# RWKV stage of a hybrid decoder layer: PSUM banks dealt out anew, and norms, joins, inversion and gate jobs placed elsewhere in the order

## The chip, the cores and the metric

One core of a Trainium2 chip runs the kernel. The metric is device time in microseconds, the median of several runs; before the change it is 2560.88 us (2558.31 to 2565.73 over 3 runs). Beside these runs there is one profiled execution, from which every row below is read.

## What is computed

One layer of a decoder over a prompt of 1040 rows and 64 sample rows: an input projection, an mLSTM mixer, an RWKV-7 mixer, a merge of the two behind gates, an output projection and a conv FFN. The change touches the RWKV mixer:

```
S = S * w + sa (kk * a) + v k        (per head, state 64 x 64; sa = S . -kk)
y = S r
y = headnorm(y) * lnx_g + lnx_b + (sum r k r_k) v      (the "bonus")
hB = y * g                                             (gate from a LoRA)
merged = sigmoid(gA) hA + sigmoid(gB) hB
```

The reference steps through time one row after another; the kernel works in chunks of 64 rows, where the delta rule becomes a triangular system per head and chunk whose inverse is computed on VectorE.

## The kernel before

Phase 1 does norms, mLSTM and its projections, phase 2 the output projection and the FFN. Between them lies the recurrent stage, the method `rwkv`, some 1250 us long. Its rows come in three passes of 384 columns, its 16 heads in four groups of 4 (two head pairs, 128 partitions each): 12 steps `(pas, u)`. A loop n runs over the steps, from -2 to 12. In one turn of it, four things are laid side by side in 18 rounds:

- the chain (`rwkv_chain`) of step n: for each of 6 chunks three parts, one a round. Part one multiplies the state with the chunk's rows (`y<-S,RA`, `y<-VU,Gk`), part two solves with the inverse (`u<-Rs,TT`), and lets the next chunk's rows be transposed (`t<-cst,v`, `t<-cst,KB`), part three makes the state update (`u<-VU,KBT`) and the outputs (`y<-VU,Gr`), which DVE (L1044) adds into the state and ACT (L1046) copies into Yt.
- the preparation of step n+2 (`rwkv_g`, `rwkv_t`, `rwkv_mid`): chunk products G (`gg<-RA,KB`), read off by DVE into Gd, Gr and Gk (L809 to L818); the inversion on DVE, a chain of 30 pairs of products in LX (L842, L844) between a transpose of Gd (L835) and two of LX (T, L887 and L889); then two products with the inverse on PE (`gg<-T,A`), each in two halves, P1 with P2 and P3 with P4 here. Each generator yields the time, in turns, at which it wants to go on; those numbers (`t0` for the inversion, `m0` for the products) set where the work stands. Steps that open a pass are n = 0, 4 and 8 of the 12.
- the rear of step n-1 (`rwkv_back`): head norm, transposes (`t<-cst,Yt`), merge.
- dense projections, in units of three matmuls (hi x hi, lo x hi, hi x lo, `d<-X..`), 8 units to a job: k and r of step n+2 (`rwkv_k`, `rwkv_r`), v of step n+1, and gate jobs from one queue (`gates_b`, `gate_o`, `gate_a`). The list `ga` says how many gate jobs each turn takes, from n = -2 on. Small pieces (the gate's LoRA product, the bonus products) wait in the list `small` and are let in some units later.

PE's order is as the code is written (a manual schedule); a scheduler orders the other engines by priority. `rwkv_r` also makes the norm of kk on PE (`y<-cst,sq`) and the decay products on DVE.

PSUM has 8 banks: two `d` for dense work, one `t` for transposes, two `y` and one `u` for the chain, the norm, bonus and gate pieces, and one double bank `gg` for chunk products. The method `gbank` hands out `gg`; a new tile waits until the readers of the last one are done.

Of the kernel before, what the change touches and what calls it, by code (L numbers as in the profile page):

```python
# [14 lines left out]
P = 128  # L15
# [28 lines left out]
class Trunk:  # L44
# [89 lines left out]
    def setup(self):  # L134
        nc, tc, ctx, i = self.nc, self.tc, self.ctx, self.i
        self.cpool = ctx.enter_context(tc.tile_pool(name="cpool", bufs=1))
        self.dram = ctx.enter_context(tc.tile_pool(name="dram", bufs=1, space=bass.MemoryType.DRAM))
        self.wpool = ctx.enter_context(tc.tile_pool(name="wpool", bufs=1))
        self.psd = ctx.enter_context(tc.tile_pool(name="psd", bufs=2, space=bass.MemoryType.PSUM))
        self.pst = ctx.enter_context(tc.tile_pool(name="pst", bufs=1, space=bass.MemoryType.PSUM))  # L140
        self.psc = ctx.enter_context(tc.tile_pool(name="psc", bufs=1, space=bass.MemoryType.PSUM))
        c = self.cpool
        self.cst = c.tile([P, NCONST], F32, name="cst")
        self.xs_d = self.dram.tile([9, P, D], F32, name="xs_d")
        self.mA_d = self.dram.tile([8, P, 1152], F32, name="mA_d")
        self.gA_d = self.dram.tile([8, P, 1152], F32, name="gA_d")
        self.gB_d = self.dram.tile([8, P, 1152], F32, name="gB_d")
        self.o_d = self.dram.tile([8, P, 706], F32, name="o_d")
        self.x_d = [self.dram.tile([P, KT, 1114], F32, name=n) for n in ("xh_d", "xl_d")]
        self.mg_d = self.dram.tile([8, P, 1152], F32, name="mg_d")  # L150
# [80 lines left out]
    def gbank(self):  # L231

        self.complete()
        return self.psg.tile([P, 2, 512], F32, name="gg")

# [397 lines left out]
    def gates_b(self, pas, j, w, pool):  # L633

        nc, i = self.nc, self.i
        off = W * pas
        lw = self.wpool.tile([P, 512], F32, name="raw", bufs=3)[:, 0:128]
        nc.sync.dma_start(out=lw, in_=i["lora2"][j, :, 256:384])
        lh = pool.tile([P, 128], F32R, name="lwgh")
        ll = pool.tile([P, 128], F32R, name="lwgl")  # L640
        self.parts(lw, lh, ll, nc.gpsimd)
        th = pool.tile([P, W], F32, name="tho", bufs=3)
        yield from self.tanh_gate(pas, w, th)
        xg = self.xg

        def piece():
            ps = self.psc.tile([P, 512], F32, name="y", bufs=2)
            self.mm3(ps[:, :W], (lh, ll), xg, True, True)
            nc.vector.scalar_tensor_tensor(th, th, 1.0, ps[:, :W], op0=ALU.add, op1=ALU.mult)
            nc.sync.dma_start(out=self.gB_d[j, :, off:off + W], in_=th)  # L650

        self.small += [(self.cfg.get("b1", 4), piece)]
# [45 lines left out]
    def rwkv_r(self, pas, j, w, pool):  # L698
# [7 lines left out]
        act = nc.scalar.activation  # L706
        st = self.st[pas, j]
        r, k, a, b, lw = (st[n] for n in ("r", "k", "a", "b", "lw"))
        cw, Dt, ta = (pool.tile([P, W], F32, name=n) for n in ("cw", "Dt", "ta"))
# [33 lines left out]
        yield from units  # L743

        n2 = r_["n2"]
        ps = self.psc.tile([P, 512], F32, name="y", bufs=2)
        for p in range(NP):
            self.mm(ps[:, 2 * p:2 * p + 2], sq[:, p * 128:(p + 1) * 128], self.const("bones2"))
        c = slice(6 * m, 6 * m + 6)
        ts(n2[:, c].rearrange("p (h n) -> p n h", h=2), ps[:, 0:6].rearrange("p (n h) -> p n h", h=2), 1e-24, None, op0=ALU.max)  # L750
        nc.vector.reciprocal(n2[:, c], n2[:, c])
        if m:
            n2L = pool.tile([P, 32], F32, name="n2L", bufs=2)
            nc.vector.transpose(n2L, n2)
        yield
        DL = pool.tile([P, 16], F32, name="DL", bufs=6)
# [9 lines left out]
        tt(r, r, Dv, op=ALU.mult)  # L766
        st["DL"] = DL
        if m:
            self.un[pas, j // 2] = dict(n2L=n2L)
# [58 lines left out]
    def rwkv_t(self, pas, u, pool):  # L828
# [4 lines left out]
        g = self.r["Gd"][:, 0:384]  # L833
        yield self.cfg.get("t0", 0.87)
        nc.vector.transpose(LX, bass.AP(g.tensor, g.offset, [list(g.ap[0]), [12, 32], [1, 32]]))  # L835
        tt(LX, LX, n2L.unsqueeze(2).broadcast_to([P, 32, 32]), op=ALU.mult)
        nc.gpsimd.memset(LX.rearrange("p t s -> p (t s)")[:, 0:1024:33], 1.0)
        for s in range(1, 31):
            m = 31 - s
            tm = pool.tile([P, 240], F32, name="tm")  # L840
            tv_ = tm[:, 0:m * s].rearrange("p (t s) -> p t s", s=s)
            tt(tv_, LX[:, s + 1:, s:s + 1].broadcast_to([P, m, s]),  # L842
               LX[:, s:s + 1, 0:s].broadcast_to([P, m, s]), op=ALU.mult)
            tt(LX[:, s + 1:, 0:s], LX[:, s + 1:, 0:s], tv_, op=ALU.add)  # L844
            if s % 2 == 0:
                yield self.cfg.get("t0", 0.87) + self.cfg.get("tw", 0.75) * s / 30
        tt(LX, LX, n2L.unsqueeze(1).broadcast_to([P, 32, 32]), op=ALU.mult)
        yield self.cfg.get("t0", 0.87) + self.cfg.get("tw", 0.75)

    def rwkv_bonus(self, pas, j, pool):  # L850
# [13 lines left out]
        def piece():  # L864
            ps = self.psc.tile([P, 512], F32, name="y", bufs=2)
            for x in (hi, lo):
# [10 lines left out]
    def rwkv_mid(self, pas, u, pool):  # L877
# [5 lines left out]
        cs = slice(0, 12)  # L883
        m0 = self.cfg.get("m0", 1.78) if (pas, u) != (0, 0) else self.cfg.get("m00", 1.78)
        yield m0
# [3 lines left out]
        nc.vector.transpose(Tn, LX.rearrange("p t s -> p s t"))  # L889
        yield m0 + 0.1  # L890
        P1 = A21
# [20 lines left out]

        yield from (m0 + 0.12 for _ in product(A21, Tn, 0, 32, lambda w, h1: nc.scalar.copy(P1[h1], w[h1])))
        for q in (0, 64):
            nc.scalar.copy(TT[q:q + 32, 0, :, cs], Tx[q:q + 32, :, cs])
        nc.scalar.copy(TT[:, 1, :, cs], Tx[:, :, cs])
        yield m0 + 0.15
        yield from (m0 + 0.17 for _ in product(P1, Tx, 32, 0, lambda w, h0: nc.scalar.copy(
            TT[h0, 1, :, cs].rearrange("p t c -> p c t"), w[h0])))
        if pas == 0:  # L920

            yield m0 + 0.2
            for m, st in self.pairs(pas, u):
# [16 lines left out]
    def rwkv_chain(self, pas, u, pool):  # L940
# [30 lines left out]
        for p in range(NP):  # L971
            nxt = []
            for e in range(2):
# [5 lines left out]
                if not (smp or meta):  # L979
                    for m, st in prs:  # L980
                        sd = pool.tile([P, 128], F32, name="SD", bufs=4)
                        nc.scalar.activation(sd, S2[m], AF.Copy, scale=st["DL"][:, ch:ch + 1])
                        SD.append(sd)
                yr = self.psc.tile([P, 512], F32, name="y", bufs=2)
                yy, rr = yr[:, 0:128], yr[:, 128:256]
# [17 lines left out]
                yield  # L1003
                up = self.psc.tile([P, 512], F32, name="u")
                for h in range(2):
                    for m in range(2):
                        self.mm(up[brs[m], hh[h]], TT[brs[m], :, :, 6 * m + h * NP + p], Rs[brs[m], hh[h]])
                for m in range(2):
                    nc.scalar.copy(now[m][0][brs[m], e, :], up[brs[m], 0:128])
                if p + 1 < NP:  # L1010
# [12 lines left out]
                else:  # L1023
                    sp = self.psc.tile([P, 512], F32, name="u")
                    for m in range(2):
                        for h in range(2):
                            self.mm(sp[hh[h], 64 * m:64 * m + 64], now[m][1][:, e, hh[h]], now[m][0][:, e, hh[h]], skip=True)
                for h in range(2):
# [117 lines left out]
    def rwkv(self, steps):  # L1146

        self.st, self.un, self.tho, self.mt, self.rest = {}, {}, {}, {}, None
        i, N = self.i, len(steps)
# [21 lines left out]
        queue = [x for n in range(N) for x in gates(n)]  # L1171
        share = self.cfg.get("ga", [0] + [6] * 8 + [5, 5, 5, 9, 0, 0])

# [72 lines left out]
        for n in range(-2, N + 1):  # L1246
# [13 lines left out]
            for r in range(rounds):  # L1260
                if r == 12 and 0 <= n + 1 < N:
                    self.rwkv_bonus(steps[n + 1][0], 2 * steps[n + 1][1], pool)
# [4 lines left out]
                for m, x in inside.items():  # L1267
                    now = n + r / rounds - (m - 2)
                    while x[0] <= now and "n2L" in self.un.get(steps[m], ()):
                        x[0] = next(x[1], 9)  # L1270
                        if m in starts and x[0] < self.cfg.get("t0", 0.87):
                            x[0] = max(x[0], now + self.cfg.get("id", 0.05))
# [19 lines left out]
    def phase1(self, early, p1, rs):  # L1292
        tc, nc = self.tc, self.nc
        self.rs = rs
        self.normed = {}
        with tc.tile_pool(name="psg1", bufs=2, space=bass.MemoryType.PSUM) as self.psg, tc.tile_pool(name="m", bufs=1) as mp:
            self.mp = mp
# [32 lines left out]
        self.lo_eng = nc.gpsimd  # L1330
        with tc.tile_pool(name="psg2", bufs=1, space=bass.MemoryType.PSUM) as self.psg:
            with tc.manual_schedule(engines={mybir.EngineType.PE}):
# [3 lines left out]
    def phase2(self, early):  # L1336
# [3 lines left out]
        NX = 1090  # L1340
        with tc.tile_pool(name="psg3", bufs=2, space=bass.MemoryType.PSUM) as self.psg, tc.tile_pool(name="p2", bufs=1) as pp:
            X1h = pp.tile([P, KT, NX], F32R, name="X1h")
# [384 lines left out]
```

## Time and profile before

| What | Value |
|---|---|
| Median of 3 runs | 2560.88 us |
| The profiled execution | 2566.45 us, span 2564.7 us |
| PE busy, share of the span | 2385.6 us, 93% |
| DVE, ACT, POOL busy | 1549.9, 1085.7, 476.1 us |
| Mean granted clock of TensorE | 0.96 of full speed |

Busy times add up an engine's instructions; matmuls overlap, so PE's busy share says where it stood still rather than how full it was. The granted clock is a share of 2.4 GHz; it has two levels, 1.2 and 2.4 GHz, and a mean between them says how long each held.

### The profile page before, as it was taken

The page shows a single profiled execution, that of the slowest core. Times are in us where ns is not written, and L with a number is a line of the kernel's source. Part 1 is how long each engine was busy: PE and PEld are TensorE (multiplying, and loading weights), DVE is VectorE, ACT ScalarE, POOL GpSimd, SP SyncE. Part 2 cuts the span into 40 slices and gives each one's busy share as a digit, 9 for nine tenths or more (in the row PEclk, how much of TensorE's full clock was granted, in tenths as well). Part 3 has the DMA queues.
Part 4 walks back from the last instruction along what each step waited for, and adds up shares of the span by engine and source line. Part 5 has one row for each costly group of instructions (what it writes and reads, how often), then busy time and mean ns, then how long its engine had stood idle before and what let it go on. Part 6 is the DMA issues. An engine that isn't in the chain of part 4 may idle for free. (4 is left out here: it accounts for less than half of the span.)

```text
span 2564.7 us, 43729 instructions
## 1 busy us (share of the span) xinstructions
PE 2385.6 (93%) x16303; PEld 2148.3 (84%) x16303; DVE 1549.9 (60%) x3367; ACT 1085.7 (42%) x2454; POOL 476.1 (19%) x669
## 2 busy tenths in 40 slices
PE   6999998879899899999989999989999999999997
PEld 5888897768787788888878888888999999999996
DVE  7654545888885588765688874356434333343437
ACT  4443444435444456545646655445313222132222
POOL 5100014444553211101111212221000000000003
PEclk9998998889999899999999999989999999999999
DMA  8562534435448354557445566895211111021112
GB/s 277 174 174 82 181 122 127 161 122 174 132 155 262 110 167 158 175 176 247 143 159 163 165 205 212 267 318 181 62 29 62 36 47 47 32 63 33 50 38 81
DMA packets 212508, 356.97 MB, mean 139 GB/s; under 512 B 24626, under 2 KB 83890, under 8 KB 212295
## 3 DMA queue, kind: packets, MB, share of 16 engines
q1 hardware_dynamic: 212295, 354.17, 43.0%
q8 instruction: 129, 2.11, 0.3%
q14 instruction: 84, 0.69, 0.1%
HBM read 272.00 MB, written 82.08 MB: 138 GB/s over the span
## 5 line engine op out<-in xcount | busy, mean ns | idle before, releaser
L57 PE MATMUL d<-Xh,whi 128*128 128x384 f32 (+3 forms) x1544 | 557.8, 361 | 12.4 <-ACT sm L1142 3.7
L57 PE MATMUL d<-Xl,whi 128*128 128x384 f32 (+3 forms) x1544 | 531.0, 344 | 1.4 <-DMA Xl<-xl_d 0.9
L57 PE MATMUL d<-Xh,wlo 128*128 128x384 f32 (+3 forms) x1544 | 529.1, 343 | 2.4 <-DMA wlo<-lo_w_out_b 1.4
L57 PE MATMUL d<-X1h,whi 128*128 128x364 f32 (+2 forms) x1120 | 371.1, 332 | 3.5 <-ACT whi L90 3.4
L57 PE MATMUL d<-X1h,wlo 128*128 128x364 f32 (+2 forms) x1120 | 370.7, 331 | 0.0
L57 PE MATMUL d<-X1l,whi 128*128 128x364 f32 (+2 forms) x1120 | 370.2, 331 | 0.0
L57 PEld LDWEIGHTS d<-Xh,whi 128*128 128x128 f32 (+1 forms) x1544 | 302.3, 196 | 37.6 <-issue 8.8
L57 PEld LDWEIGHTS d<-Xl,whi 128*128 128x128 f32 (+1 forms) x1544 | 303.0, 196 | 6.1 <-DMA Xl<-xl_d 4.1
L57 PEld LDWEIGHTS d<-Xh,wlo 128*128 128x128 f32 (+1 forms) x1544 | 301.9, 196 | 5.5 <-DMA wlo<-lo_w_out_b 2.3
L73 ACT CAST whi<-raw 128x512 fp32r<-128x512 f32 (+1 forms) x255 | 157.0, 617 | 336.7 <-PE d L57 273.3
L57 PEld LDWEIGHTS d<-X1h,whi 128*128 128x128 f32 x1120 | 212.1, 189 | 8.0 <-ACT whi L90 3.9
L57 PEld LDWEIGHTS d<-X1l,whi 128*128 128x128 f32 x1120 | 212.0, 189 | 4.9
L57 PEld LDWEIGHTS d<-X1h,wlo 128*128 128x128 f32 x1120 | 212.2, 189 | 3.3
L90 ACT CAST whi<-raw 128x512 fp32r<-128x512 f32 x232 | 142.9, 618 | 137.5 <-PE d L57 75.7
L1550 DVE TENSOR_TENSOR acc<-y,acc 128x512 f32<-128x512 f32 (+1 forms) x144 | 97.6, 687 | 169.9 <-PE y L57 169.9
L74 POOL TENSOR_TENSOR wlo<-raw,whi 128x512 fp32r<-128x512 f32 x120 | 163.3, 1362 | 186.0 <-ACT whi L73 167.7
L74 DVE TENSOR_TENSOR wlo<-raw,whi 128x512 fp32r<-128x512 f32 (+1 forms) x135 | 97.0, 722 | 153.4 <-ACT whi L73 152.1
L844 DVE TENSOR_TENSOR LX<-LX,tm 128x30 f32<-128x30 f32 (+4 forms) x360 | 148.4, 412 | 9.8 <-DVE tm L842 0.5
L57 PE MATMUL y<-wdh,hh 128*128 128x512 f32 x352 | 138.9, 395 | 4.8 <-DVE acc L1550 4.8
L842 DVE TENSOR_TENSOR tm<-LX 128x30 f32<-128x30 f32 (+4 forms) x360 | 137.9, 383 | 8.8
L57 PE MATMUL y<-wdl,hh 128*128 128x512 f32 x352 | 138.4, 393 | 0.0
L57 PE MATMUL y<-wdh,hl 128*128 128x512 f32 x352 | 138.3, 393 | 0.0
(364 smaller groups left out, 4199.2 us busy)
## 6 DMA issues: line engine op xcount, KB each, us to landing
raw<-in_w_up_dram SPq DMA_DIRECT2D x88, 256.0 KB, 2.8
raw<-in_wv_dram SPq DMA_DIRECT2D x48, 256.0 KB, 3.3
raw<-in_wk_b_dram SPq DMA_DIRECT2D x48, 256.0 KB, 4.0
raw<-in_wr_dram SPq DMA_DIRECT2D x48, 256.0 KB, 3.1
raw<-in_wv_b_dram SPq DMA_DIRECT2D x48, 256.0 KB, 3.4
raw<-in_wgb_dram SPq DMA_DIRECT2D x48, 256.0 KB, 3.7
raw<-in_wo_dram SPq DMA_DIRECT2D x48, 256.0 KB, 3.3
raw<-in_wga_dram SPq DMA_DIRECT2D x48, 256.0 KB, 3.2
```

Source lines behind the costliest of these rows:

```text
L57: self.nc.tensor.matmul(out, lhsT, rhs, start=start, stop=stop, skip_group_check=skip)
L73: nc.scalar.copy(hi[:, :n], src[:, u:u + n])
L74: self.lo_eng.tensor_tensor(lo[:, :n], src[:, u:u + n], hi[:, :n].bitcast(F32), op=ALU.subtract)
L90: nc.scalar.copy(hi, raw)
L842: tt(tv_, LX[:, s + 1:, s:s + 1].broadcast_to([P, m, s]), LX[:, s:s + 1, 0:s].broadcast_to([P, m, s]), op=ALU.mult)
L844: tt(LX[:, s + 1:, 0:s], LX[:, s + 1:, 0:s], tv_, op=ALU.add)
L1550: tt(acc[0:m, t, ns], ps[0:m], acc[0:m, t, ns], op=ALU.add)
```

## The change

- Banks: within the recurrent stage there is one `y` bank, no `u`, and two double `gg` banks. The solved rows (`up`) and the state update (`sp`) of a chunk take the third and fourth quarter of its y bank. Norm, bonus and gate pieces use the one `t` bank. The pool `psc` is opened anew in each phase.
- `rwkv_r` first lets the waiting small pieces in, does the decay products right behind r, and the norm one unit later; the bonus isn't begun while it is in between.
- The inversion's time `t0` goes from 0.87 to 0.79, that of the products `m0` from 1.78 to 1.72, and each half product and join gets a round of its own.
- Gate jobs: `ga` is dealt out otherwise, with the same total of 72.

```
-        self.psc = ctx.enter_context(tc.tile_pool(name="psc", bufs=1, space=bass.MemoryType.PSUM))
...
-        return self.psg.tile([P, 2, 512], F32, name="gg")
+        return self.psg.tile([P, 2, 512], F32, name="gg", bufs=2)
...
         def piece():
-            ps = self.psc.tile([P, 512], F32, name="y", bufs=2)
+            ps = self.pst.tile([P, 512], F32, name="t")
...
         st = self.st[pas, j]
+        while self.small:
+            self.small.pop(0)[1]()
+        self.within = True
...
         tt(r, r, Dv, op=ALU.mult)
         st["DL"] = DL
+        self.within = False
+        yield
+
+        n2 = r_["n2"]
+        ps = self.pst.tile([P, 512], F32, name="t")
+        for p in range(NP):
+            self.mm(ps[:, 2 * p:2 * p + 2], sq[:, p * 128:(p + 1) * 128], self.const("bones2"))
...
-        yield self.cfg.get("t0", 0.87)
+        yield self.cfg.get("t0", 0.79)
...
-        m0 = self.cfg.get("m0", 1.78) if (pas, u) != (0, 0) else self.cfg.get("m00", 1.78)
+        m0 = self.cfg.get("m0", 1.72) if (pas, u) != (0, 0) else self.cfg.get("m00", 1.72)
...
-        yield m0 + 0.1
+        yield m0 + 0.055
...
-        yield from (m0 + 0.12 for _ in product(A21, Tn, 0, 32, lambda w, h1: nc.scalar.copy(P1[h1], w[h1])))
+        yield from (m0 + 0.11 for _ in product(A21, Tn, 0, 32, lambda w, h1: nc.scalar.copy(P1[h1], w[h1])))
...
-        yield m0 + 0.15
-        yield from (m0 + 0.17 for _ in product(P1, Tx, 32, 0, lambda w, h0: nc.scalar.copy(
+        yield m0 + 0.165
+        yield from (m0 + 0.22 for _ in product(P1, Tx, 32, 0, lambda w, h0: nc.scalar.copy(
...
-            yield m0 + 0.2
+            yield m0 + 0.23
...
-                yr = self.psc.tile([P, 512], F32, name="y", bufs=2)
+                yr = self.psc.tile([P, 512], F32, name="y")
...
-                up = self.psc.tile([P, 512], F32, name="u")
+                up, sp = yr[:, 256:384], yr[:, 384:512]
...
-                        self.mm(up[brs[m], hh[h]], TT[brs[m], :, :, 6 * m + h * NP + p], Rs[brs[m], hh[h]])
+                        self.mm(up[brs[m], hh[h]], TT[brs[m], :, :, 6 * m + h * NP + p], Rs[brs[m], hh[h]], meta, True, True)
...
-        share = self.cfg.get("ga", [0] + [6] * 8 + [5, 5, 5, 9, 0, 0])
+        share = self.cfg.get("ga", [0, 9, 6, 6, 3, 7, 7, 7, 3, 5, 5, 5, 9, 0, 0])
...
-                if r == 12 and 0 <= n + 1 < N:
+                if r >= 12 and 0 <= n + 1 < N and "bon" not in self.st[steps[n + 1][0], 2 * steps[n + 1][1]] and not self.within:
```

What this moves in the engines' order, at three places. On PE, in the second step of pass 1, the half products of the inverse (`gg<-T,A`) before the change, among dense matmuls (`d`) and the chain (`u`, `y`); lines of dense matmuls are left out:

```order
L57 MATMUL u<-VU,KBT 64x64 x4
L57 MATMUL y<-VU,Gr 64x64 x4
L57 MATMUL gg<-T_11720,A_10088 32x32 x12
L57 MATMUL gg<-T_11718,A_10088 32x32 x12
L57 MATMUL d<-Xh,whi 128x384
...
L57 MATMUL gg<-T_11718,A_10088 32x32 x12
L57 MATMUL y<-S_4211,RA 64x128 x4
```

The second half of the first product and the first half of the second stood next to each other. At the same place of the program afterwards, on PE:

```order
L57 MATMUL y<-S_4212,RA 64x128 x4
L57 MATMUL y<-VU,Gk 64x64 x4
L57 MATMUL gg<-T_11641,A_10098 32x32 x12
L57 MATMUL d<-Xh,whi 128x384
...
L57 MATMUL y<-Rs,TT_4228 64x64 x4
L960 MATMUL t<-cst,v 128x128
L962 MATMUL t<-cst,KB 128x128 x2
L57 MATMUL gg<-T_11639,A_10098 32x32 x12
L57 MATMUL d<-Xh,whi 128x384
```

Between the two there are now 18 dense matmuls and the solve. The second place is the end of a chunk on ACT, before the change, with what each instruction waits for (the copy of the outputs is `Yt<-y`, the next chunk's scaled state `SD`):

```order
L345 ACTIVATE tho<-d 128x384 [waits DMAHW4_49,PE_49]
L90 CAST whi<-raw 128x512 [waits DMAHW3_49,PE_49,Activation_49]
L1046 COPY Yt<-y 128x128 [waits PE_49]
L982 ACTIVATE SD<-S_4211,DL 128x128 [waits DVE_49] x2
L982 ACTIVATE SD<-S_4211,DL 128x128 x2
```

Afterwards on ACT, at such an end of a chunk:

```order
L344 ACTIVATE tho<-d 128x384 [waits DMAHW5_49,PE_49]
L985 ACTIVATE SD<-S_4212,DL 128x128 [waits DVE_49]
L1048 COPY Yt<-y 128x128 [waits DVE_49,PE_49]
L985 ACTIVATE SD<-S_4212,DL 128x128
L985 ACTIVATE SD<-S_4212,DL 128x128 [waits Activation_49] x2
```

The copy stands behind DVE's state update now, and behind a scaling that needs it. The third place is a bonus behind the transposes on PE, before the change:

```order
L57 MATMUL u<-Rs,TT_4224 64x64 x4
L957 MATMUL t<-cst,v 128x128
L959 MATMUL t<-cst,KB 128x128 x2
L57 MATMUL y<-cw,ones 128x384
L57 MATMUL y<-Dt,ones 128x384
```

And afterwards on PE:

```order
L57 MATMUL y<-Rs,TT_4228 64x64 x4
L960 MATMUL t<-cst,v 128x128
L962 MATMUL t<-cst,KB 128x128 x2
L57 MATMUL t<-cw,ones 128x384
L57 MATMUL t<-Dt,ones 128x384
```

The bonus writes the bank that the transposes have just filled and that ACT has yet to read.

## Rows read from the trace of the kernel before

**Rows 1.** Busy time of each engine in the recurrent stage, with granted clock.
```profile
440.00:1690.00 1250.00, 1143.40 (x9323) 1007.44 (x9324) 909.66 (x2104) 640.54 (x1571) 328.29 (x441) 0.95 0.56 178
```

**Rows 2.** Whom PE waited for, 440 to 1690: total us, times, longest.
```profile
PE gg L57 <- DVE Gk L818: 30.9, 16, 3.9
PE gg L57 <- DVE T L889: 17.7, 3, 14.5
PE gg L57 <- ACT A L913: 12.7, 12, 1.1
PE y L57 <- ACT sq L733: 9.9, 2, 5.2
PE y L57 <- POOL T L934: 4.5, 3, 2.5
...
PE gg L57 <- DVE S L1038: 2.8, 1, 2.8
...
PE y L57 <- DVE S L1044: 0.9, 4, 0.4
```

**Rows 3.** Time line of PE: start, us, line, operation, out, in, shapes, idle before.
```profile
452.86 0.71 PE L57 MATMUL gg<-RA,KB 64*128 64x128 f32 x8 [1.84 <-DVE Gk L818]
453.51 0.43 PE L57 MATMUL d<-Xh,whi 128*128 128x346 f32 x1
...
457.86 0.32 PE L57 MATMUL d<-Xh,wlo 128*128 128x346 f32 x1
...
512.35 0.32 PE L57 MATMUL d<-Xh,whi 128*128 128x346 f32 x1
...
517.52 0.32 PE L57 MATMUL d<-Xh,wlo 128*128 128x346 f32 x1
532.30 0.87 PE L57 MATMUL gg<-T,A 32*32 32x32 f32 x24 [14.46 <-DVE T L889]
```

**Rows 4.** Busy PE, PEld, DVE, ACT, POOL and clock between LX's and T's transposes.
```profile
477.73:532.24 54.51, 35.71 (x218) 33.08 (x216) 52.46 (x111) 16.38 (x39) 21.82 (x26) 0.85 0.51 167
905.29:961.82 56.53, 52.60 (x416) 46.76 (x414) 51.45 (x126) 28.63 (x72) 7.33 (x15) 1.00 0.58 180
1276.53:1332.96 56.43, 49.65 (x390) 43.94 (x388) 50.97 (x125) 27.76 (x73) 5.09 (x11) 0.96 0.52 172
```

**Rows 5.** The wait for Gk: 440 to 532.24, 880 to 961.82, 1276.53 to 1332.96.
```profile
PE gg L57 <- DVE Gk L818: 9.6, 6, 3.0
...
PE gg L57 <- DVE Gk L818: 5.8, 3, 3.0
...
PE gg L57 <- DVE Gk L818: 3.3, 2, 3.2
```

**Rows 6.** Time line of POOL and DVE in the first inversion.
```profile
483.52 1.28 POOL L74 TENSOR_TENSOR wlo<-raw,whi 128x512 fp32r<-128x512 f32 x1 [0.63 <-ACT whi L73]
...
483.66 1.21 DVE L844 TENSOR_TENSOR LX<-LX,tm 128x30 f32<-128x30 f32 x1
...
485.16 0.22 DVE L844 TENSOR_TENSOR LX<-LX,tm 128x58 f32<-128x58 f32 x1
```

**Rows 7.** Time line of PE, DVE and ACT at the end of one chunk.
```profile
1134.81 0.40 PE L57 MATMUL y<-VU,Gr 128*64 128x64 f32 x8
...
1135.02 1.20 DVE L1044 SCALAR_TENSOR_TENSOR S<-u,DL,SD 64x64 f32<-64x64 f32 x4
...
1135.26 0.27 ACT L1046 COPY Yt<-y 128x128 f32<-128x128 f32 x1
1135.64 0.40 ACT L982 ACTIVATE SD<-S,DL 128x128 f32<-128x128 f32 x1
...
1137.98 0.66 PE L57 MATMUL y<-S,RA 128*64 128x128 f32 x8
```

**Rows 8.** Time line of PE and ACT behind one chunk's transposes.
```profile
1005.44 0.38 PE L959 MATMUL t<-cst,KB 128*128 128x128 f32 x2
...
1006.40 0.37 ACT L965 COPY KBT<-t 128x256 f32<-128x256 f32 x1
```

More of the change, by code (lines that the diff above doesn't have):

```diff
@@ L743, in rwkv_r @@
         yield from units
[L745 to L755, printed above, removed]
         DL = pool.tile([P, 16], F32, name="DL", bufs=6)
@@ L767, in rwkv_r @@
         st["DL"] = DL
+        self.within = False
[4 more added lines that the diff above has]
+            self.mm(ps[:, 2 * p:2 * p + 2], sq[:, p * 128:(p + 1) * 128], self.const("bones2"))
+        c = slice(6 * m, 6 * m + 6)
+        ts(n2[:, c].rearrange("p (h n) -> p n h", h=2), ps[:, 0:6].rearrange("p (n h) -> p n h", h=2), 1e-24, None, op0=ALU.max)
+        nc.vector.reciprocal(n2[:, c], n2[:, c])
+        if m:
+            n2L = pool.tile([P, 32], F32, name="n2L", bufs=2)
+            nc.vector.transpose(n2L, n2)
         if m:
@@ L845, in rwkv_t @@
             if s % 2 == 0:
-                yield self.cfg.get("t0", 0.87) + self.cfg.get("tw", 0.75) * s / 30
+                yield self.cfg.get("t0", 0.79) + self.cfg.get("tw", 0.75) * s / 30
         tt(LX, LX, n2L.unsqueeze(1).broadcast_to([P, 32, 32]), op=ALU.mult)
-        yield self.cfg.get("t0", 0.87) + self.cfg.get("tw", 0.75)
+        yield self.cfg.get("t0", 0.79) + self.cfg.get("tw", 0.75)
     def rwkv_bonus(self, pas, j, pool):
@@ L864, in piece @@
         def piece():
-            ps = self.psc.tile([P, 512], F32, name="y", bufs=2)
+            ps = self.pst.tile([P, 512], F32, name="t")
             for x in (hi, lo):
@@ L1003, in rwkv_chain @@
                 yield
-                up = self.psc.tile([P, 512], F32, name="u")
+                up, sp = yr[:, 256:384], yr[:, 384:512]
                 for h in range(2):
                     for m in range(2):
-                        self.mm(up[brs[m], hh[h]], TT[brs[m], :, :, 6 * m + h * NP + p], Rs[brs[m], hh[h]])
+                        self.mm(up[brs[m], hh[h]], TT[brs[m], :, :, 6 * m + h * NP + p], Rs[brs[m], hh[h]], meta, True, True)
                 for m in range(2):
-                    nc.scalar.copy(now[m][0][brs[m], e, :], up[brs[m], 0:128])
+                    nc.scalar.copy(now[m][0][brs[m], e, :], up[brs[m], :])
                 if p + 1 < NP:
@@ L1023, in rwkv_chain @@
                 else:
-                    sp = self.psc.tile([P, 512], F32, name="u")
                     for m in range(2):
                         for h in range(2):
-                            self.mm(sp[hh[h], 64 * m:64 * m + 64], now[m][1][:, e, hh[h]], now[m][0][:, e, hh[h]], skip=True)
+                            self.mm(sp[hh[h], 64 * m:64 * m + 64], now[m][1][:, e, hh[h]], now[m][0][:, e, hh[h]], meta, True, True)
                 for h in range(2):
@@ L1146, in rwkv @@
     def rwkv(self, steps):
-        self.st, self.un, self.tho, self.mt, self.rest = {}, {}, {}, {}, None
+        self.st, self.un, self.tho, self.mt, self.rest, self.within = {}, {}, {}, {}, None, False
         i, N = self.i, len(steps)
@@ L1270, in rwkv @@
                         x[0] = next(x[1], 9)
-                        if m in starts and x[0] < self.cfg.get("t0", 0.87):
+                        if m in starts and x[0] < self.cfg.get("t0", 0.79):
                             x[0] = max(x[0], now + self.cfg.get("id", 0.05))
@@ L1295, in phase1 @@
         self.normed = {}
-        with tc.tile_pool(name="psg1", bufs=2, space=bass.MemoryType.PSUM) as self.psg, tc.tile_pool(name="m", bufs=1) as mp:
+        with tc.tile_pool(name="psc1", bufs=1, space=bass.MemoryType.PSUM) as self.psc, tc.tile_pool(name="psg1", bufs=2, space=bass.MemoryType.PSUM) as self.psg, tc.tile_pool(name="m", bufs=1) as mp:
             self.mp = mp
@@ L1330, in phase1 @@
         self.lo_eng = nc.gpsimd
-        with tc.tile_pool(name="psg2", bufs=1, space=bass.MemoryType.PSUM) as self.psg:
+        with tc.tile_pool(name="psc2", bufs=1, space=bass.MemoryType.PSUM) as self.psc, tc.tile_pool(name="psg2", bufs=1, space=bass.MemoryType.PSUM) as self.psg:
             with tc.manual_schedule(engines={mybir.EngineType.PE}):
@@ L1340, in phase2 @@
         NX = 1090
-        with tc.tile_pool(name="psg3", bufs=2, space=bass.MemoryType.PSUM) as self.psg, tc.tile_pool(name="p2", bufs=1) as pp:
+        with tc.tile_pool(name="psc3", bufs=1, space=bass.MemoryType.PSUM) as self.psc, tc.tile_pool(name="psg3", bufs=2, space=bass.MemoryType.PSUM) as self.psg, tc.tile_pool(name="p2", bufs=1) as pp:
             X1h = pp.tile([P, KT, NX], F32R, name="X1h")
```

## The prediction

> **What bounds the kernel now.** I went from the stretches to the waits, and from the waits to the time line. In the recurrent stage (440 to 1690 us) TensorE is busy 1143.4 of 1250 us [rows 1], so every cure together can give back 106.6 us of idling, plus what the clock loses behind it. The reader should see that TensorE bounds the stage and that its gaps are many and short: the list of waits [rows 2] is led by the chunk-product bank (`gg` waiting for DVE's Gk, 30.9 us in 16 waits), then the inverse (T, 17.7 in 3, of which 14.46 in front of 532.30 [rows 3]), then the second half of the chunk inverse (A, 12.7 in 12, each close to the 1.1 shown as longest).
>
> The time line shows what a gap costs beyond itself [rows 3]. Dense matmuls at full speed start 0.162 us apart (32 steps from 512.35 to 517.52). After the 1.84 us wait at 452.86 the next 18 need 453.51 to 457.86, 0.256 us a step: a clock fall that costs 17 x 0.094 = 1.6 us. A wait of 1.5 us or more counts so in what follows, one near 1.05 does not.
>
> Third, who holds T. Between the transpose that starts an inversion and the T that ends it, in the three steps that open a pass, DVE is busy 52.46 of 54.51, 51.45 of 56.53 and 50.97 of 56.43 us [rows 4]. There DVE is the bound and TensorE's idling is what is left over.
>
> **The change part by part.**
>
> *Half products in rounds of their own.* Before, halves two and three stand next to each other on PE, so the third waits for the ACT copy of the first product; afterwards a round of 15 to 24 dense matmuls (2.4 us and more) stands between. The 1.05 us copy is covered: 12.7 us gone [rows 2]. If a step had no dense work there it would come back; the order shows none such.
>
> *Two double banks for chunk products.* A block of G no longer waits for the block just before it. Of the 30.9 us, 9.6 lie before 532 us, 5.8 between 880 and 962, and 3.3 in the third window [rows 5]; 12.2 us in 5 waits lie elsewhere. Those I count as gone, with some 4 us of clock: 16 (bounds 8 to 20). The waits inside the three windows give nothing: a TensorE that runs ahead there stands longer at T. The part ahead of the windows, which lets the inversion start earlier, is about half of 15.4 us: 8, and two clock falls, 11 (bounds 0 to 19; 0 if DVE, with little idle time left, can't go faster).
>
> *Inversion and joins earlier.* This is the part that hurts. Counting in the order, the dense matmuls between a pass's last G block and its first half product go from 165 to 156, 192 to 171 and 180 to 147: 63 fewer, x 0.162 = 10.2 us less work to cover windows whose length DVE sets. DVE's own operations between the two transposes are nearly the same afterwards (six blends of v fall ahead of the first window, one gate product drops out of each of the others: some 2.6 us). So 10.2 - 2.6, and a clock fall of 1.6 in the middle window, whose wait was next to nothing (17.7 less 14.46 is all that the last two have): 9 us lost (bounds 4 to 14). In the other nine steps nothing waited for T, so an earlier product costs nothing there while T has time to spare.
>
> *Gate jobs moved.* Three more jobs of 24 dense matmuls go ahead of the first chain step (nine for six), the two steps before a new pass get three for six. The dense sum stays. Before the first half product this is 21 matmuls net (375 against 354), which the counts above hold. But each job also splits two weight halves on POOL, and there DVE is the bound: where the split at 483.52 ran (1.28 us), a DVE product of 30 elements took 1.21 us, and one of 58 elements just after it 0.22 [rows 6]. One job more before T is two splits, up to 2 us, which I take out of the 11 above rather than add.
> The Trainium skill (GPSIMD Engine Reference, section 8, Key points) says that GpSimd shares its SBUF interfaces with VectorE and that DVE instructions with two SBUF inputs contend; the trace agrees, with 1.21 against 0.22 us. By that rule all six added splits would lengthen the DVE-bound opening, 6 us instead of 2, and the sum would be 4 us worse.
>
> *Norm after the decay products; banks.* The squares held TensorE 9.9 us in two waits in pass 0, behind a DVE that was in arrears with the next inversion. In the new order DVE has the second inversion mostly behind it when the norm comes, since 81 dense matmuls for 30 stand between the first half product and the chain. I take half of it and a clock fall, 6 (bounds 0 to 13). The sample masks (POOL T, 4.5) get nine dense matmuls of distance, and the sample state update (S, 2.8) a bank of its own: 5 of 7.3 (bounds 2 to 9).
>
> *Solved rows and state update in the y bank.* One bank is now written by PE, read by DVE and by ACT, and the order shows the price: 68 of 72 copies of Yt wait for DVE, the state update waits for the last y matmul, and the next step's first matmul waits for ACT. At the join at 1134.81 [rows 7] the y products end at 1135.21, the update ran from 1135.02 to 1136.22, the copy took 0.27, and the next read of the state started at 1137.98, so 1.76 us to spare. Afterwards: update from 1135.3 on (0.3 later), then the copy (0.27 plus a SD scaling of 0.40 that can stand ahead): about 1 us used, 0.8 left. So the ordinary join is covered by the 15 dense matmuls around it. 16 of the 72 have less than 1.25 us to spare, some of them waiting already (the wait for S of L1044) [rows 2], and the last step has 12 dense matmuls a round: 16 x 0.5 = 8 us lost (bounds 2 to 20).
>
> *Norms, bonus and gates in the t bank.* The single t bank had 8 users a step and gets 6 more. The transposes' last matmul ends at 1005.82 and ACT's last copy of them at 1006.77 [rows 8], so who follows at once waits 0.95 and a handover. In the order 15 users stand within 6 dense matmuls (1 us) behind another one: six bonuses and two norms behind the transposes, two bonuses behind a bonus, and five transposes behind a bonus or norm that DVE has yet to read. 15 x 0.55 = 8, and one clock fall: 10 us lost (bounds 3 to 25; the upper end if DVE reads each only after 1.5 us more).
>
> Phase 1 keeps its PE order, and behind the recurrent stage only the banks' places move: 0 (within 3).
>
> Sum: -12.7 - 16 - 11 - 6 - 5 + 9 + 8 + 10 = -23.7. The profiled execution took 2566.45 us (2564.7 span), so 2542.7; the median of the runs shown, 2560.88, is 5.6 lower than that execution, so **2537 us**.
>
> **The rivals.**
>
> *The shared y bank decides (slower).* It needs the chain update, copy, next read to be longer than the 0.8 us left by more than a little in most joins. ACT works in order, and casts of weights stand ahead of its copies as DVE's inversion products do ahead of updates. If 60% of the joins lost 1 us more than I allow, 43 us would go and the time is 2537 + 43 = 2580; it turns slower from about 32 us on, 0.75 us in 43 joins. Against it: at the join shown [rows 7] ACT began its copy at 1135.26, 0.05 us after the products' end.
> By the Trainium skill (PSUM — Partial Sum Buffer, section PSUM bank collisions raise a hardware error) no two of the three engines may be in one bank and partition at once, so the waits in the order can't be relaxed; no run here shows the collision itself.
>
> *Nothing much moves (same).* DVE is the bound over more than the three windows, and the waits only change their names, from Gk to T and to DVE's reading of the dense banks. Then 12.7 and the lower 8 of the Gk outside stay, against 27 of losses: +6 us and 2567 with all of these, 2554 with bank losses of 5 for 18; I take 2558. For it speak [rows 4]; against it that DVE is busy only 909.66 of 1250 us [rows 1].
>
> *The banks cost nearly nothing (faster still).* If DVE reads the t bank at once and the joins hold, 18 us of losses fall to 5, and the squares and the 11 come fully: 2537 - 13 - 8 = 2516.
>
> **How the numbers follow.** My sum 0.58 (2522 to 2552 by its own bounds), cheap banks 0.17, nothing much 0.15, y bank 0.10. About 0.3%, 7.7 us, is what a measurement here can tell from no change: faster means under 2553.2, same up to 2568.6. That gives faster 0.58 + 0.17 = 0.75, same 0.15, slower 0.10. The range leaves out the slow rival and the best part of the cheap one: 2514 to 2558.
>
> **What would show it.** In the waits of the changed kernel: no third row of 12 for `gg` on ACT A; Gk under 10 us; T larger than 17.7 (25 to 40 us, three waits); a new row of PE `t` on ACT KBT and on DVE's bonus (5 to 12 us); `y` on ACT Yt (3 to 12 us). The three inversion windows still 53 to 56 us long with DVE over 90% busy. I am wrong if T's waits shrink, which would mean that the windows were not DVE's, or if `y` on Yt is over 25 us, or if the time line shows dense stretches at 0.29 us a step behind waits near 1 us.

## The result, and the profile of the changed kernel

The changed kernel takes **2528.57 us** (median of 4 runs, 2522.82 to 2535.62) against 2561.45 of the kernel before beside it: ratio 0.9871, 95% interval 0.9841 to 0.9902. Timed again beside the later experiments it was 0.9890 (0.9868 to 0.9912). So 28 to 33 us are gone; 24 were forecast, and the time lies in the range.

First the page: the span, and TensorE's busy time. Before it was busy 2385.6 us of a span of 2564.7.

```profile
span 2529.8 us, 43736 instructions
PE 2361.2 (93%) x16303; PEld 2125.8 (84%) x16303; DVE 1549.8 (61%) x3367; ACT 1078.4 (43%) x2454; POOL 481.2 (19%) x669
```

The same matmuls take 24.4 us less, the idling shrinks by 10.5 only. More than half of the gain is TensorE working faster on them.

Next the stretches, first of the kernel before (window and length, then busy time and instructions of PE, PEld, DVE, ACT and POOL, then the granted clock, the DMA's busy share and GB/s): the recurrent stage from its first `gg` matmul to the first matmul of phase 2, and its two long stretches between inversion windows.

```profile
420.40:1696.00 1275.60, 1163.84 (x9424) 1025.01 (x9424) 925.23 (x2141) 655.47 (x1602) 345.26 (x480) 0.94 0.56 179
532.30:905.30 373.00, 333.99 (x2714) 290.42 (x2715) 274.93 (x590) 175.92 (x441) 150.90 (x204) 0.92 0.50 158
961.80:1276.50 314.70, 301.86 (x2540) 264.82 (x2540) 220.00 (x529) 180.46 (x436) 49.56 (x85) 0.97 0.56 180
```

The same of the changed kernel, with its three inversion windows, which answer to [rows 4]:

```profile
417.80:1658.30 1240.50, 1141.06 (x9425) 1003.28 (x9425) 928.07 (x2141) 648.74 (x1602) 351.32 (x480) 0.96 0.58 184
...
475.00:527.40 52.40, 34.21 (x208) 30.71 (x206) 50.17 (x106) 15.55 (x37) 20.33 (x22) 0.83 0.52 173
527.40:868.00 340.60, 317.09 (x2709) 274.63 (x2710) 276.67 (x588) 172.32 (x438) 152.38 (x202) 0.97 0.54 170
868.00:924.20 56.20, 46.65 (x352) 40.97 (x350) 50.86 (x125) 27.09 (x68) 5.10 (x13) 0.93 0.53 168
924.20:1233.50 309.30, 303.66 (x2588) 266.50 (x2588) 220.68 (x530) 180.01 (x440) 52.58 (x87) 0.98 0.58 185
1233.50:1287.50 54.00, 39.85 (x329) 34.79 (x328) 50.40 (x125) 24.04 (x62) 4.32 (x9) 0.94 0.49 154
```

The stage holds the whole gain: 1275.6 to 1240.5 us. The windows are about as long as they were (54.5, 56.5 and 56.4 us), with DVE busy 50.2 of 52.4, 50.9 of 56.2 and 50.4 of 54.0 us. Of the 35 us, 32 come out of one stretch in pass 0 (373.0 to 340.6), where almost the same number of matmuls runs at a clock of 0.97 instead of 0.92. The last stretch, from the third window to the end of the stage, has grown from 363.0 to 370.8 us.

The list of TensorE's waits in the stage (total, times, longest), answering to [rows 2]:

```profile
PE gg L57 <- DVE T L892: 28.3, 3, 13.6
PE y L57 <- ACT Yt L1048: 11.7, 13, 2.9
PE t L960 <- DVE n L766: 8.0, 2, 4.5
PE t L57 <- ACT KBT L968: 7.3, 8, 1.8
...
PE t L960 <- DVE bon L875: 6.0, 4, 3.5
...
PE t L57 <- DVE bon L875: 4.4, 1, 4.4
```

Gk (30.9) and A (12.7) are gone altogether, T has grown from 17.7 to 28.3, and four rows of waits for the one `t` bank, 25.7 us in all, stand in the place of the squares.

Executions of one kernel differ: those of before beside the experiments lie between 2547.6 and 2570.5 us. Part of that is phase 1, which the change leaves alone. The stretch from 200 to 240 us in two executions of the changed kernel, the first profile and then that of run 5:

```profile
200.00:240.00 40.00, 38.61 (x231) 32.16 (x230) 22.03 (x61) 14.79 (x41) 1.37 (x3) 1.00 0.32 91
```

```profile
200.00:240.00 40.00, 38.54 (x202) 32.42 (x202) 18.37 (x51) 14.36 (x40) 1.37 (x3) 0.84 0.31 89
```

So below the verdicts come from the timed ratios, and the places from the stage alone. The stage of a single profile can be off too: 1240.5 and 1242.1 us in these two, but in runs 1, 4 and 7 of the table below it is 10 to 18 us shorter than before although the whole kernel takes the same time. The profile of run 1 is the fastest of ten executions, 9.5 us under their median, and the one of before is 5.6 above the median of its three. A difference in the stage counts here when it is larger than that, or comes again in a second pair of runs.

### The profile page after: what moved, and what is told of

The parts are those of the page before. It is cut to its first block, busy times and chain, and to the rows that moved or that the text cites. A ratio compares the mean times of both kernels' runs of the same rounds, so it can differ in the third digit from the quotient of the medians.

```text
span 2529.8 us, 43736 instructions
## 1 busy us (share of the span) xinstructions
PE 2361.2 (93%) x16303; PEld 2125.8 (84%) x16303; DVE 1549.8 (61%) x3367; ACT 1078.4 (43%) x2454; POOL 481.2 (19%) x669
## 4 chain that ended last, share of the span: by engine, by line
PE 48%; DVE 5%; DMA 4%; ACT 1%; issue 1%; SPq 0%; POOL 0%; DVEq 0%; ACTq 0%
PE d L57 33%; PE y L57 12%; PE gg L57 2%; DMA mg_d<-mA 1%; DVE acc L128 1%; PE t L57 1%; DMA tho<-mA_d 1%; DMA raw<-mg_d 0%; DVE S L1046 0%; DVE Gd L812 0%; DMA mA<-gA_d 0%; DVE tm L845 0%; DVE acc L1552 0%; PE t L960 0%; DVE LX L847 0%
## 5 line engine op out<-in xcount | busy, mean ns | idle before, releaser
L57 PE MATMUL d<-X1h,wlo 128*128 128x364 f32 (+3 forms) x1120 | 370.8, 331 | 0.0
L57 PE MATMUL d<-X1l,whi 128*128 128x364 f32 (+3 forms) x1120 | 370.0, 331 | 0.0
L74 POOL TENSOR_TENSOR wlo<-raw,whi 128x512 fp32r<-128x512 f32 x120 | 163.2, 1362 | 154.2 <-ACT whi L73 96.9
```

The source lines that it names most:

```text
L57: self.nc.tensor.matmul(out, lhsT, rhs, start=start, stop=stop, skip_group_check=skip)
L74: self.lo_eng.tensor_tensor(lo[:, :n], src[:, u:u + n], hi[:, :n].bitcast(F32), op=ALU.subtract)
```

## The experiments

All are timed against the kernel before on the same chip (9 to 12 on another one than 1 to 8); PE busy and the clock are of the stage, bounded as above.

| kernel | ratio (95%) | stage us | PE busy | clock |
|---|---|---|---|---|
| before | 1 | 1275.6 | 1163.8 | 0.94 |
| changed | 0.9871 (0.9841–0.9902) | 1240.5 | 1141.1 | 0.96 |
| 5 changed, again | 0.9890 (0.9868–0.9912) | 1242.1 | 1143.7 | 0.96 |
| 1 banks alone | 1.0001 (0.9979–1.0023) | 1257.9 | 1152.8 | 0.95 |
| 2 order alone | 0.9903 (0.9875–0.9931) | 1245.7 | 1146.1 | 0.96 |
| 3 changed, one chunk bank | 0.9950 (0.9926–0.9974) | 1264.2 | 1148.6 | 0.96 |
| 4 changed, halves adjacent | 1.0014 (0.9990–1.0037) | 1263.8 | 1158.0 | 0.95 |
| 6 the same without the wait | 0.9877 (0.9853–0.9901) | 1246.0 | 1142.0 | 0.96 |
| 7 inversion's times alone | 0.9994 (0.9977–1.0010) | 1265.1 | 1156.1 | 0.94 |
| 8 small users in `gg` | 0.9851 (0.9826–0.9876) | 1229.2 | 1138.9 | 0.96 |
| 9 order with old gates | 1.0004 (0.9986–1.0022) | 1274.3 | 1158.8 | 0.94 |
| 10 changed, old gates | 1.0014 (0.9998–1.0030) | 1273.9 | 1155.7 | 0.95 |
| 11 as 8, start 1 round later | 0.9858 (0.9832–0.9884) | 1231.4 | 1142.0 | 0.96 |
| 12 as 8, start 2 rounds later | 0.9807 (0.9783–0.9832) | 1216.8 | 1133.5 | 0.97 |

**1. The banks alone**: the kernel before with the new pools; due times, gate shares, norm and bonus start are old.

```diff
-        return self.psg.tile([P, 2, 512], F32, name="gg")
+        return self.psg.tile([P, 2, 512], F32, name="gg", bufs=2)
...
-            ps = self.psc.tile([P, 512], F32, name="y", bufs=2)
+            ps = self.pst.tile([P, 512], F32, name="t")
...
-                up = self.psc.tile([P, 512], F32, name="u")
+                up, sp = yr[:, 256:384], yr[:, 384:512]
```

> The kernel before with the new banks alone: order of norms, bonus start, inversion times and gate jobs as before. By the terms of the prediction for banks (Gk -16 and -11, sample update and masks -5, y bank +8, t bank +10) it is 14 us faster, ratio 0.9945 to the kernel before; the row of gg on Gk falls under 10 us, the 12 waits of gg on A stay near 12.7 us. Rival (the single t bank decides once norms and bonuses stand in it in the old places): t waits on DVE and ACT of 40 us and more, ratio 1.000 or above. Rival (short waits also lower the clock): ratio 0.990, with TensorE's busy time 10 us or more under before's 2385.6.

Measured 1.0001: no gain. TensorE's waits there:

```profile
PE gg L57 <- DVE T L888: 17.9, 2, 16.0
PE y L57 <- ACT Yt L1044: 13.1, 11, 2.7
PE t L956 <- DVE bon L871: 8.7, 5, 3.0
PE gg L57 <- ACT A L912: 8.6, 20, 1.3
PE t L956 <- DVE n L749: 8.3, 2, 6.0
...
PE t L57 <- ACT KBT L964: 7.4, 9, 1.2
```

Of Gk 0.9 us are left, but the waits have new names: 13.1 on Yt, and 24.4 in the three `t` rows shown. The rival that the `t` bank decides in the old order is the nearest, though it had named 40 us.

**2. The order alone**: the changed kernel on the banks of before (edit 1 the other way round).

> The changed kernel with the banks of before (chunk products single, y double, u apart): only order and times are new. By the terms of the prediction (half products -12.7, squares -6, inversion and joins +9) 10 us faster, ratio 0.996; gg on Gk stays at 25 to 35 us, gg on A is gone. Rival (waits of about 1 us lower the clock too): 17 us or more faster, ratio 0.993, TensorE busy 8 us less than before. Rival (the single chunk bank holds the earlier half products up, the waits only change name): ratio 0.999 to 1.002, with Gk or A copies above 40 us.

0.9903, more than either of the first two sizes: the order carries most of the gain by itself. Gk still costs 20.2 us there, T 31.2.

**3. One double bank for chunk products** in the changed kernel (`bufs=1` in `gbank`; the two banks stay empty).

> The changed kernel with one double bank for chunk products; the two freed banks stay empty, so y and t keep their new users. By the prediction's terms for the second double bank (16 and 11) 27 us are lost: ratio 0.998 to the kernel before, gg on Gk 25 to 35 us. Rival (the second double bank is worth little, the gain is that of the order): ratio under 0.991. Rival (each Gk wait also costs clock): ratio 1.002 or more, TensorE busy 10 us above that of the changed kernel (2361.2).

0.9950: 15 to 20 us against the changed kernel, 22 to 24 in the stage. Gk stands at 12.9 us in 11 waits, and the first inversion starts 67.7 us into the stage instead of 57.2. Beside a `t` bank that already has its new users, the second chunk bank is worth somewhat less than the 27 of the prediction, and half of it lies ahead of the first window, as argued. What the whole set of new banks gives there is less; the section on the prediction comes back to it.

**4 and 6. Half products two and three side by side**, and the same where the third waits for no copy.

```diff
-        yield m0 + 0.165
-        yield from (m0 + 0.22 for _ in product(P1, Tx, 32, 0, lambda w, h0: nc.scalar.copy(
+        yield m0 + 0.105
+        yield from (m0 + 0.165 for _ in product(P1, Tx, 32, 0, lambda w, h0: nc.scalar.copy(
```

Run 6 has `A21, Tx, 0, 0` for the second product's operands and rows on top of that, and the first product is copied into `Tn`; it leaves out the off-diagonal block of the inverse.

> The changed kernel with half products two and three next to each other again (due times 0.105 and 0.165 for 0.165 and 0.22), all else as changed. By the prediction's term 12.7 us are lost, in 12 waits of about 1.05 for ACT's copy of the first product: ratio 0.992 to the kernel before. Rival (a wait of 1.05 us is followed by low clock in a third of the cases, as before's rows at 843, 968, 1234 and 1582 us seem to show): 19 to 20 us lost, ratio 0.995, and TensorE busy 6 to 8 us above 2361.2. Rival (TensorE waits elsewhere for what it gained here): under 5 us lost, ratio under 0.989, with T or t waits smaller by 8 us.

> Half products two and three next to each other as in the kernel that lost the whole gain (1.0014), but the third reads A itself instead of the first product (and writes a block that the inverse doesn't need), so it waits for no copy; the off-diagonal block of the inverse is thereby left out. If the wait is the price (0.79 us of idling in two pieces, twelve times, and what lies behind), it is back at 0.988. If the stretch of some 50 small matmuls without a dense one is the price, by the clock behind it, it stays at 0.996 or more, with about 12 slow dense steps behind six and more of the twelve pairs. Between the two (0.990 to 0.994) both count.

The waits came back at 9.5 us in 24 pieces, as forecast, but the whole gain went: 1.0014. One of the twelve pairs in run 4, from TensorE's time line (start, duration, matmul, and in brackets the wait ahead of it):

```profile
1040.00 0.85 PE L57 MATMUL gg<-T,A 32*32 32x32 f32 x24
1041.42 0.28 PE L57 MATMUL gg<-T,A 32*32 32x32 f32 x2 [0.57 <-ACT A L916]
1041.92 0.84 PE L57 MATMUL gg<-T,A 32*32 32x32 f32 x22 [0.22 <-ACT A L916]
1042.69 0.69 PE L57 MATMUL d<-Xh,whi 128*128 128x384 f32 x1
1043.18 0.52 PE L57 MATMUL d<-Xl,whi 128*128 128x384 f32 x1
1043.50 0.52 PE L57 MATMUL d<-Xh,wlo 128*128 128x384 f32 x1
...
1046.20 0.34 PE L57 MATMUL d<-Xh,wlo 128*128 128x384 f32 x1
1046.38 0.34 PE L57 MATMUL d<-Xh,whi 128*128 128x384 f32 x1
```

And the same pair in run 6:

```profile
1019.14 1.31 PE L57 MATMUL gg<-T,A 32*32 32x32 f32 x48
1020.38 0.44 PE L57 MATMUL d<-Xh,whi 128*128 128x384 f32 x1
1020.66 0.34 PE L57 MATMUL d<-Xl,whi 128*128 128x384 f32 x1
1020.84 0.34 PE L57 MATMUL d<-Xh,wlo 128*128 128x384 f32 x1
```

In run 4 the dense matmuls behind the pair start 0.32 us apart, from 1046.20 on 0.18; the granted clock from 1042.6 to 1049.0 is 0.74. Of the nine pairs outside the opening steps five have some ten such slow starts behind them (clock 0.70 to 0.76 over the next 5 to 7 us). In run 6 as many small matmuls stand without a dense one between them, none of the nine has such a stretch behind it (clock 1.00 from 1020.3 to 1027.0), and the time is back at 0.9877. So it is the wait, short as it is, and not the stretch of small matmuls. The stage differs by 18 us between the two runs, of which TensorE's busy time has 16. The timed medians differ by 33; the rest isn't placed: in the two profiles 11 us of it lie ahead of the stage, where the edits change nothing.

**7. The inversion's times alone**: the kernel before with `t0` 0.79, `m0` 1.72 and the five new offsets.

> The kernel before with the new due times of the inversion and its half products alone (banks, norms, gates as before). By the terms of the prediction -12.7 +9 = -4 us, ratio 0.9985. If the half products apart carry the whole gain of the order (the run with order alone gave 0.9903), 0.990 to 0.992. If gates and norms carry the rest, 0.995 to 0.998, with squares holding TensorE about 10 us as before.

0.9994. A is gone, and T has taken its place, in the list of waits:

```profile
PE gg L57 <- DVE T L889: 35.6, 3, 16.0
PE gg L57 <- DVE Gk L818: 27.3, 15, 3.2
```

**9 and 10. The gate jobs of before**, in the order alone (9) and in the changed kernel (10).

```diff
-        share = self.cfg.get("ga", [0, 9, 6, 6, 3, 7, 7, 7, 3, 5, 5, 5, 9, 0, 0])
+        share = self.cfg.get("ga", [0] + [6] * 8 + [5, 5, 5, 9, 0, 0])
```

> Order alone on the banks of before (0.9903), now with the gate jobs of before too: what stays new is the inversion's due times and the norm behind the decay products. If the moved gate jobs carry what the inversion's times alone did not give (0.9994), 0.996 to 1.000, with T waits at 35 us as in the run with the inversion's times alone. If the norm's move carries it, 0.990 to 0.992.

> The changed kernel with the gate jobs of before. By the prediction (the dense sum stays, some 0 to 2 us either way) 0.987 to 0.989. If the moved gate jobs are worth 20 us, 0.995 to 0.998, most of it in the long stretch of pass 0 between the first inversion window's end and the second's start (340.6 us in the changed kernel, 373.0 before).

1.0004 and 1.0014: without the moved gate jobs nothing is left, in either set of banks. The windows that follow count only the dense bank `d` (length, PE busy and matmuls first, clock third from the end). They run from the stage's start to the last Yt copy of step 0, then over step 2, steps 4 and 5, and step 6. First run 10:

```profile
421.50:642.10 220.60, 128.77 (x672) 115.34 (x672) 15.34 (x62) 14.22 (x38) 0.89 0.49 155
739.50:848.50 109.00, 63.76 (x312) 54.76 (x312) 4.47 (x13) 7.35 (x21) 0.92 0.61 195
964.80:1141.90 177.10, 112.53 (x580) 100.55 (x578) 8.60 (x22) 12.71 (x24) 0.99 0.54 174
1141.90:1238.20 96.30, 65.94 (x312) 57.30 (x312) 4.20 (x10) 7.34 (x14) 0.95 0.65 207
```

Then the changed kernel:

```profile
417.80:642.40 224.60, 139.51 (x744) 126.94 (x744) 15.15 (x62) 15.76 (x44) 0.91 0.54 170
741.80:828.40 86.60, 48.99 (x240) 40.77 (x240) 5.23 (x15) 6.01 (x15) 0.98 0.65 206
945.90:1123.90 178.00, 122.22 (x627) 107.94 (x626) 8.53 (x22) 13.75 (x26) 1.00 0.59 188
1123.90:1200.10 76.20, 48.70 (x243) 41.46 (x241) 4.95 (x12) 5.98 (x11) 1.00 0.67 218
```

Here is a failed step. Steps 2 and 6, which come two steps ahead of a new pass, lose 72 and 69 dense matmuls and 22.4 and 20.1 us. The stretch to the end of step 0 gets 72 and is 4.0 us longer, steps 4 and 5 get 47 and are 0.9 longer. At 0.162 us, 72 matmuls are 11.7 us; they cost less than that where TensorE had idle or slow time to fill, and gave back more where they went. In steps 2 and 6 most of what came back is busy time of TensorE, all banks counted (96.9 to 80.1 and 90.9 to 72.7 us), at a clock that rose from 0.92 to 0.98 and from 0.95 to 1.00; why fewer dense matmuls leave the clock higher there isn't shown. The other pair, run 9 and then run 2, says the same: 20.8 and 16.1 us back in steps 2 and 6, 1.6 more to the end of step 0, 3.0 more in steps 4 and 5.

What the first stretch pays is DVE's. The three jobs more bring six splits on POOL, five of them ahead of the first T (31 against 26). The inversion's two operations from the stage's start to that T, in run 10 (count, busy us and mean ns):

```profile
L847 DVE TENSOR_TENSOR LX<-LX,tm 128x30 f32<-128x30 f32 (+14 forms) x30 | 12.6, 420 | 0.8
L845 DVE TENSOR_TENSOR tm<-LX 128x30 f32<-128x30 f32 (+14 forms) x30 | 11.3, 375 | 0.8
```

and in the changed kernel:

```profile
L847 DVE TENSOR_TENSOR LX<-LX,tm 128x30 f32<-128x30 f32 (+14 forms) x30 | 16.1, 538 | 0.8
L845 DVE TENSOR_TENSOR tm<-LX 128x30 f32<-128x30 f32 (+14 forms) x30 | 12.4, 413 | 0.8
```

This part lasts 109.6 us against 102.6, with DVE busy 97.3 against 92.0. I had allowed up to 2 us. The two operations together take 28.5 us against 23.9, and in the other pair (2 against 9) 27.7 against 25.0, with the part 4.5 us longer. The slow ones are those that run while POOL is busy: 18 of the 60 in run 10 and 21 in the changed kernel, which lose 4.2 and 8.8 us against the shortest time of the same shape, while the others lose 0.1 and 0.2 us in all. The number of splits isn't the whole of it: in the kernel before, with the old gate jobs and 29 splits, 25 ran beside POOL and lost 8.8 us too, and its part lasts 111.8 us. The rule of the Trainium skill (GPSIMD Engine Reference, section 8, Key points), that VectorE and GpSimd contend when the DVE instruction has two SBUF inputs, agrees with this trace in kind; the 6 us that the prediction worked out by it stand against 4.6 and 2.7 in the two operations and 7.0 and 4.5 in the part.

**5 and 8. The changed kernel again; norms, bonuses and gates in the chunk banks** (`ps = self.gbank()[:, 0, :]` for the `t` tile in the three places).

> The changed kernel once more, beside the next three, so that they are compared on one chip: 0.984 to 0.990 of the kernel before, as first measured.

> The changed kernel with norms, bonuses and gates in the two double chunk banks instead of the t bank. If the t bank costs what its waits show (8.0 on the norm, 10.4 on the bonus, 4.4 on gate inputs, about half of the 7.3 on KBT), up to 20 us come back and the ratio is 0.980 to 0.983. If they only change their name (to gg on the norm and the bonus, or to T, where DVE bounds), 0.986 to 0.988. If the chunk blocks are held up by them, Gk or A waits come back: 0.990 and more.

0.9851 beside 0.9890: about 10 us, 11 to 13 in the stage; the intervals touch, but the executions don't overlap (2519 to 2525 against 2530 to 2536 us). That is what these users cost on the `t` bank, with part of it waiting under other names, in the list of waits of run 8:

```profile
PE gg L57 <- DVE T L892: 29.0, 3, 13.2
PE y L57 <- ACT Yt L1048: 12.6, 16, 2.1
...
PE gg L57 <- ACT sq L735: 5.0, 3, 3.7
...
PE gg L57 <- DVE bon L875: 3.3, 1, 3.3
```

**11 and 12. Half products later in the opening steps**, on top of 8; 12 has 1.83 for 1.775.

```diff
-        m0 = self.cfg.get("m0", 1.72) if (pas, u) != (0, 0) else self.cfg.get("m00", 1.72)
+        m0 = 1.775 if u == 0 else 1.72
```

> The kernel with norms, bonuses and gates in the chunk banks (0.9851), and in the three steps that open a pass the half products one round later (due time 1.775 for 1.72), so that 15 to 21 dense matmuls more stand ahead of the first. If DVE sets the windows, the waits for T (29.0 us in three) fall by 15 to 21 x 0.162, 2.4 to 3.4 us each: 20 us left, ratio 0.9815 to 0.983. Rival (the work is missing behind T, where something else waits, or the inverse comes too late for the solved rows): 0.985 or above, with new waits on TT or A.

> The same two rounds later (due time 1.83): 33 to 45 matmuls more ahead of T, 5.3 to 7.3 us a window, the last two half products side by side at the step's end (they don't wait for each other). If DVE sets the windows, T waits of 10 to 13 us in all, ratio 0.978 to 0.981. Rival (the inverse comes too late): solved rows wait for TT, 1 to 3 us in each of three places and a clock fall behind each: 0.983 to 0.986.

One round later took 7 us off T (22.0) and nothing measurable off the time: that expectation missed. T fell in the second and third window only; in the first it is 14.3 against 13.2 in run 8, and the stretch to the end of step 0 is 10 us longer in this profile, which eats what steps 3 and 7 gain (9.5 and 6.8). Two rounds later gave 0.9807, the best of all, some 49 us under before and 11 under run 8 (each beside its own runs of the kernel before). In its list of waits T is halved, and what is left is nearly all the first window's:

```profile
PE gg L57 <- DVE T L892: 15.1, 2, 12.3
```

No new wait for TT stands in that list, so the rival falls.

## Why the prediction was right, and by which of its steps it was not

Sign and size came out, the sum behind them did not: two gains set far too small (half products, gates) made up for two set too large (banks, norm). That the total still came out is luck.

**Half products: mis-sized.** -12.7 was the waits alone. Undoing it costs 23 us of stage and the whole gain in the timed runs (4). The step that failed is "a wait of 1.5 us or more counts so in what follows, one near 1.05 does not". It was read from [rows 2, 3] without looking behind each of the twelve waits: in the kernel before, dense matmuls start 0.32 us apart behind the wait of 1.05 us at 968.54, with a clock of 0.72 from 968.5 to 974.5. Run 4 shows the sign that the prediction had named against itself, slow dense stretches behind short waits.

**Gate jobs: wrong.** "The dense sum stays" put the move at nothing beside 2 us for POOL's splits, and so took a dense matmul to cost the same in every step. Moving them is worth 26 us in the one pair of runs (9 against 2) and 32 to 37 in the other (10 against the changed kernel). I had only counted whether they cover T and what they split, and at T they helped too: 35.6 to 36.6 us without them (7, 9, 10), 28.3 and 31.2 with them (the changed kernel, 2).

**Banks: right in kind, too large in sum.** The prediction's bank terms come to -14 (-16 -11 -5 +8 +10). In the old order the banks give nothing (1), with the old gates nothing either (10 against 9), and in the new order the difference of 0.9903 to 0.9871 or 0.9890 is within the intervals. Of the 11 us that I had ahead of the windows, the new banks save 3 to 4 in each of three pairs with the same gate jobs (57.3 to 53.2 us to the first inversion from before to 1, 56.8 to 53.5 from 9 to 10, 60.2 to 57.2 from 2 to the changed kernel); the 10.5 of (3) are the price of one chunk bank beside a crowded `t`. In the changed kernel the opening is no shorter than before (57.2 and 57.3 us), since the added gate jobs take their place. `y` on Yt came at the upper end of the 3 to 12 us that I named (11.7), against a term of 8. The `t` bank was set at 10: moving its small users brings back 10 to 13 (8), and the rows for KBT and the bonus, named at 5 to 12, are 17.7, with another 8.0 for the norm. The price of the shared banks can be seen in the stage's last stretch, behind the third T: 360 to 364 us with the old banks (before, 2, 7, 9), 366 to 375 with the new ones (changed, 1, 3 to 6, 10), 359 to 363 once the small users have left `t` (8, 11, 12).

**Norm: not borne out.** -6 for the squares (9.9). In the changed kernel 8.0 us wait for `n`, which is the same norm read by DVE; with the old gates the order alone leaves squares at 10.4 (9), with the new ones at 6.9 (2). The norm's move was not run by itself.

**Inversion earlier: right.** +9; T rose by 17.9 with the times alone (7), and putting the opening steps back two rounds gave 11 (12). The windows are DVE's as [rows 4] said. Run 11 doesn't fit a simple trade of matmuls for waits, and why the stretch to the end of step 0 grew there stays open.

**The rivals.** That waits only change their names is what happened with the banks alone, but not as that rival had it: T stayed at 17.9 (17.7 before), and the waits went to the `t` and `y` banks. The `y` bank did not decide. That the banks cost nearly nothing was wrong as well.

What also stays open is how the parts combine: taking either the gate jobs or the distance of the halves out of the changed kernel costs all of the gain, so the sizes above are those beside the other parts and don't add up. The gate jobs alone, and the norm's old place with the new banks, weren't tried.

## What to carry to other kernels

A matmul has no price of its own: before saying that moved work sums to nothing, count idle and slow time of the bounding engine in each step it leaves and each it enters. A wait between small matmuls should be priced with the slow stretch behind it, looked up wait by wait. New banks gave nothing here until the order and the neighbours in the shared bank changed too, so banks and order are to be tried together.

## What the runs showed of the hardware

First, two waits of 0.57 and 0.22 us among 48 small matmuls were enough in five of nine cases for some ten dense starts at 0.32 us instead of 0.18 (0.29 instead of 0.16 in pass 0), with a granted clock of 0.70 to 0.76; without the waits it happened in none of nine. The Trainium skill (TensorE: Matmul & The Clock Gate, Part 1) lists an idle state of 1.2 and a busy one of 2.4 GHz, the throttle being released by activity; the two distances agree with two such states. Second, the same 40 us of phase 1 had a granted clock of 1.00 and 0.84 in two executions of one kernel, so a difference of ten us between two single profiles proves nothing. Third, the inversion's two DVE operations are slow only beside POOL: in the changed kernel 21 of 60 lost 8.8 us, the other 39 lost 0.2.
